# A fixed matmul order for the linear-recurrence stage of a hybrid diffusion layer

## The chip, the cores and the metric

The kernel runs on one core of a Trainium2 chip. The metric is the device time of one execution in microseconds (us); the time before is the median of three runs. Engines are named as the profile does: PE (TensorE matmul), PEld (TensorE weight load), DVE (VectorE), ACT (ScalarE), POOL (GpSimd), SP (the queue that issues DMAs).

## The reference

One transformer-like layer (DEPTH 1, model width 1024) is applied to 128 context tokens and 512 latent tokens that share all weights, so T = 640 tokens. A combined input projection feeds four mixers; the first, an HGRN2 gated linear recurrence in both directions with 4 heads of 128 x 128, is the one that this change is about:

```
q = silu(u['hgrn_q']); v = u['hgrn_i']; f = lb + (1 - lb) * sigmoid(f_pre); k = (1 - lb) * sigmoid(-f_pre)
# per chunk, b = cumsum(log f):
A = einsum('bthk,bshk,btshk->bhts', q, k, exp(b_t - b_s))       # s <= t
o = A @ v + (q * exp(b)) @ S
S = exp(b_last) * S + (k * exp(b_last - b))^T @ v
o = rmsnorm(o_fwd + o_bwd) * silu(u['hgrn_g'])
```

The other mixers are windowed attention, latent attention and grouped-query attention; each is projected to the model width, weighted by sigmoid gates of its own (a projection of 1024 columns per branch), and a squared-ReLU MLP follows. The final context states of the recurrence are outputs too.

## The kernel before, in words

All weights are split into a high part (fp32r) and a remainder, and so are the activations: a dense product is three matmuls. `t_block` (L322) makes a transposed block, 128 output channels by 640 tokens in two halves of 320, 8 x 3 matmuls per half (L330 to L332), in one of two `mm` PSUM buffers; `tok_block` (L335) makes a block of 128 tokens by 256 or 512 channels (L341 to L343). `wtile` (L289) loads a weight tile of 128 x 1024, copies its high part on POOL (`copy_r`, L124, tile wh) and subtracts on DVE (`rest`, L127, tile wl); raw, high and low parts have three buffers each.

The linear-recurrence stage works on two pairs of heads (hp = 0, 1), and all 640 tokens at once:

- `hgrn_project(hp)` (L406): the query projection (evacuated by L412 on ACT and L413 on DVE) and the forget gates of both directions (L423 and L424 on ACT, L426 and L430 on DVE, L428 on POOL). Six blocks of 48 matmuls.
- `hgrn_levels` (L437): the matrix A by recursion. It begins with QP = q * f (L441, DVE) and KS (L446, POOL) and a group of 32-wide blocks on PE (L459). Then for h = 1, 2, 4, 8, 16: a copy into KS on ACT (L468), a group of blocks (L459), and the update of the running products: QP on DVE (L485), the keys hk on POOL (L488, one per direction), the gates hf on DVE (L489); the blocks are merged under a mask (L491). For h = 32 and 64 the blocks are L478 and their results are copied to A (L495).
- `hgrn_out(hp, ...)` (L503): transposes of the keys (L515), copied by ACT (L517); the state updates u in groups of eight matmuls into two PSUM buffers (L522), chained on DVE (L527), with the final context state copied out by ACT (L530); the outputs po from A and the states (L543, L546, L547); squares (L551), the mean and its power -1/2 (L189, L190), the gated result (L559), its transposes (L561) and the split result (L566, L567).
- `hgrn_gate(hp)` (L583): the output gate, five `tok_block`s of 24 matmuls of 256 columns (L588, L589).
- `gates(n)` (L569): the branch gate, eight `t_block`s.

Blocks, key transposes and outputs share two `sc` PSUM buffers; the state updates and the result's transposes share two `tp` buffers. Behind the stage comes the windowed attention, whose key and value projections are `tok_block`s into `sc` buffers.

The order of instructions on each engine is chosen by a planner that simulates the program with a table of costs: at each moment it takes, among the instructions that are ready, the one of the highest priority, which is the order in which the program states them unless `high_priority` raises it. Tiles get a buffer when one is free. The stage is stated so:

```
qfk = hgrn_project(0)
lev = hgrn_levels(*qfk, hx)
qfk = hgrn_project(1)
hgrn_gate(0)
with tc.high_priority():
    hgrn_out(0, *lev, hV, hG, hx)
hgrn_gate(1)
sig0 = gates(0)
with tc.high_priority():
    lev = hgrn_levels(*qfk, hx)
    hgrn_out(1, *lev, hV, hG, hx)
```

Of the kernel before, what the change touches and what calls it, by code (L numbers as in the profile page):

```python
# [64 lines left out]
def trunk(ctx, tc, I, O):  # L65
    nc = tc.nc
    V, S, G, PE = nc.vector, nc.scalar, nc.gpsimd, nc.tensor
    dma = nc.sync.dma_start

# [219 lines left out]
    def wtile(rows, k0, c0, n, nk):  # L289
# [12 lines left out]
        copy_r(hi[:, 0:m], raw[:, 0:m])  # L302
# [3 lines left out]
    wtile.side = 0  # L306

# [98 lines left out]
    def hgrn_project(hp):  # L406
        qa = big(F32, 4, T, name="qA")
# [7 lines left out]
        fg = big(F32, 2, 2, T, name="hf")  # L415
        kk = big(F32, 2, 2, T, name="hk")
        for d, nm in enumerate(('hff', 'hfb')):
# [12 lines left out]
            V.tensor_scalar(out=fg[:, 1 - d], in0=fg[:, 1 - d], scalar1=LOG_FLOOR, scalar2=None, op0=ALU.max)  # L430
        return qa, fg, kk
# [5 lines left out]
    def hgrn_levels(qa, fg, kk, hx):  # L437
# [25 lines left out]
        flat = lambda x: lambda t: x.rearrange("p m t -> p (m t)")[:, t:t + 32]  # L463
        L = blocks(flat(KS), flat(q))
        V.tensor_tensor(out=AD, in0=L, in1=eye32.unsqueeze(1).to_broadcast([128, 10, 32]), op=ALU.mult)
        for li, h in enumerate(LEVELS):
            if h < 32:
                S.activation(out=skip(KS, 0, (2 * h, n2 // (2 * h)), (h, 2), (1, h)), in_=cross(kk, 0, n2 // (2 * h), h),  # L468
                             func=AF.Copy)
                L = blocks(flat(KS), lambda t: cross(QP, t, 16 // h, h))  # L470
            else:

                L = sc_tile()[:, :, 0:5 * h].rearrange("p m (c t) -> p m c t", t=h)
# [22 lines left out]
            if h == 16:  # L496
# [3 lines left out]
        return (qa, A, [QP[:, 1 - d] for d in range(2)], [kk[:, d] for d in range(2)],  # L500
                [[fg[:, 1 - d, m] for m in range(2)] for d in range(2)])

    def hgrn_out(hp, qa, A, QP, KR, P, hV, hG, hx):  # L503
        need = {0: [0, 1, 2, 4], 1: [3, 2, 1, 4]}
        st = hx.tile([128, 4, 4, 128], F32, tag="St", name="St")
        for d in range(2):
            for m in range(2):
                hd = 2 * hp + m
                dma(out=st[:, 2 * d + m, 0], in_=I['state_hgrn'][0, 0, d, hd])
        for d in range(2):  # L510
            kt_ps = sc_tile().rearrange("p m (j s) -> p m j s", j=4)
            kts = []
            for m in range(2):
                for j, c in enumerate(need[d]):
                    PE.transpose(out=kt_ps[:, m, j], in_=KR[d][:, m, 128 * c:128 * c + 128], identity=ident)  # L515
                kts.append(small(name="kt").rearrange("p (j s) -> p j s", j=4))
                S.activation(out=kts[m], in_=kt_ps[:, m], func=AF.Copy)  # L517
            for m in range(2):
                hd, kt = 2 * hp + m, kts[m]
# [5 lines left out]
                for j in range(3):  # L525
                    c = need[d][j]
                    V.scalar_tensor_tensor(out=s0[:, j + 1], in0=s0[:, j], scalar=P[d][m][:, 128 * c + 127 * d:128 * c + 127 * d + 1],  # L527
                                           in1=u[:, 128 * j:128 * j + 128], op0=ALU.mult, op1=ALU.add)
# [6 lines left out]
        on = qa[:, 0:2].rearrange("p m t -> p (m t)").rearrange("p (i v) -> p i v", v=128)  # L535
        for cs in ((4,), (0, 1, 2, 3)):
# [18 lines left out]
            for m in range(2):  # L555
                hd = 2 * hp + m
                tp = tp_tile()
                for i, c in enumerate(cs):
                    V.scalar_tensor_tensor(out=on[:, 2 * c + m], in0=po[:, 2 * i + m], scalar=r[:, 2 * i + m:2 * i + m + 1],  # L559
                                           in1=hG[:, c, 128 * hd:128 * hd + 128], op0=ALU.mult, op1=ALU.mult)  # L560
                    PE.transpose(out=tp[:, i], in_=on[:, 2 * c + m], identity=ident)  # L561
                gain = vcol[:, 40 + hd:41 + hd]
                t = slice(128 * cs[0], 128 * cs[-1] + 128)
                src = tp[:, 0:len(cs)].rearrange("p i t -> p (i t)")
                hi, lo = (x[:, t] for x in OT[0][hd])
                S.activation(out=hi, in_=src, func=AF.Copy, scale=gain)  # L566
                V.scalar_tensor_tensor(out=lo, in0=src, scalar=gain, in1=f(hi), op0=ALU.mult, op1=ALU.subtract)  # L567

    def gates(n):  # L569

# [11 lines left out]
    with tc.tile_pool(name="hx", bufs=1) as hx:  # L582
# [14 lines left out]
        with tc.high_priority():  # L597
            hgrn_out(0, *lev, hV, hG, hx)
# [590 lines left out]
```

## Time and profile before

| | |
|---|---|
| median of 3 runs | 1521.66 us (1520.61 to 1524.54) |
| the profiled execution | 1524.19 us, span 1522.4 us, mean granted clock 0.987 |
| PE busy | 1443.2 us, 95% of the span |
| PEld busy | 1309.7 us, 86% |
| DVE busy | 801.6 us, 53% |
| ACT busy | 459.8 us, 30% |
| POOL busy | 478.8 us, 31% |
| chain that ended last | PE 69%, issue 14%, DVE 7%, POOL 6%, DMA 2%, ACT 2% |

Busy is the time in which an engine has an instruction under way; a wait is the idle time just ahead of an instruction, put down to what released it. Matmuls overlap, so the start of one to the start of the next is the pace, and its own duration is longer. The granted clock is TensorE's, as a share of full speed.

### The profile page before, as it was taken

How to read it: one execution, taken by the hardware profiler on the slowest of the kernel's cores; microseconds unless marked ns; L12 is line 12 of the kernel's file. 1: busy time of each engine (PE TensorE's matmuls, PEld its weight loads, DVE VectorE, ACT ScalarE, POOL GpSimd, SP SyncE). 2: the span in 40 equal slices, each digit the busy share in tenths (PEclk: the TensorE clock that was granted, in tenths of full speed). 3: DMA queues.
4: the chain of work that ended last, by engine and by line, in shares of the span. 5: the costliest groups of instructions: out<-in, count | busy, mean ns of one | idle time of the engine just before them, and what ended most of it. 6: DMA issues, size and time to landing. Idle time of an engine off the chain costs nothing.

```text
span 1522.4 us, 26814 instructions
## 1 busy us (share of the span) xinstructions
PE 1443.2 (95%) x10970; PEld 1309.7 (86%) x10970; DVE 801.6 (53%) x1459; ACT 459.8 (30%) x1158; POOL 478.8 (31%) x506
## 2 busy tenths in 40 slices
PE   5998898999999899999998988998999999999996
PEld 3798898999899898899997677887897998998995
DVE  3337767347753497542734467756333444444446
ACT  3322232333434234442123565315220110110112
POOL 2226738232322344321323344124211112112114
PEclk9999999999999999999999999999999999999998
DMA  9422212223112230112323701231334132212221
GB/s 296 139 70 57 52 48 64 64 60 70 44 43 46 58 70 15 50 39 54 93 66 115 257 31 43 74 107 56 92 116 125 58 95 84 80 63 80 70 70 70
DMA packets 140410, 121.18 MB, mean 80 GB/s; under 512 B 22432, under 2 KB 121596, under 8 KB 140288
## 3 DMA queue, kind: packets, MB, share of 16 engines
q1 hardware_dynamic: 140288, 119.47, 27.0%
q8 instruction: 86, 1.41, 0.4%
q14 instruction: 36, 0.29, 0.1%
HBM read 115.96 MB, written 3.49 MB: 78 GB/s over the span
## 4 chain that ended last, share of the span: by engine, by line
PE 69%; issue 14%; DVE 7%; POOL 6%; DMA 2%; ACT 2%; SPq 0%; POOLq 0%; DVEq 0%; ACTq 0%
PE mm L330 11%; PE mm L331 11%; PE mm L332 11%; POOL wh L124 4%; PE mm L341 4%; PE mm L342 4%; PE mm L343 4%; PE tp L706 3%; PE sc L341 3%; PE pv L859 3%; PE sc L343 3%; PE sc L342 2%; PE sc L799 2%; PE sc L800 2%; DMA wada<-in_w_ada 1%
## 5 line engine op out<-in xcount | busy, mean ns | idle before, releaser
L124 POOL TENSOR_SCALAR wh<-wr 128x1024 fp32r<-128x1024 f32 (+3 forms) x161 | 193.4, 1203 | 583.1 <-PE mm L331 325.1
L127 DVE TENSOR_TENSOR wl<-wr,wh 128x1024 fp32r<-128x1024 f32 (+3 forms) x161 | 199.7, 1242 | 180.3 <-POOL wh L124 179.8
L330 PE MATMUL mm<-hTh,wh 128*128 128x320 f32 x704 | 221.9, 315 | 3.6 <-DVE qA L413 2.2
L332 PE MATMUL mm<-hTh,wl 128*128 128x320 f32 x704 | 221.9, 315 | 1.3 <-DVE wl L127 1.2
L331 PE MATMUL mm<-hTl,wh 128*128 128x320 f32 x704 | 220.6, 313 | 0.0
L331 PE MATMUL mm<-h2Tl,wh 128*128 128x320 f32 x512 | 159.3, 311 | 0.9 <-DVE h2Tl L127 0.9
L330 PE MATMUL mm<-h2Th,wh 128*128 128x320 f32 x512 | 159.2, 312 | 0.0
L332 PE MATMUL mm<-h2Th,wl 128*128 128x320 f32 x512 | 159.1, 311 | 0.0
L659 POOL TENSOR_SCALAR P<-P,rden 128x640 f32<-128x640 f32 (+3 forms) x120 | 83.2, 703 | 177.6 <-DVE rden L671 75.7
L330 PEld LDWEIGHTS mm<-hTh,wh 128*128 128x128 f32 x704 | 133.8, 190 | 5.8 <-DVE qA L413 2.3
L332 PEld LDWEIGHTS mm<-hTh,wl 128*128 128x128 f32 x704 | 133.8, 190 | 2.9 <-DVE wl L127 1.8
L331 PEld LDWEIGHTS mm<-hTl,wh 128*128 128x128 f32 x704 | 133.7, 190 | 0.7 <-issue 0.3
L342 PE MATMUL mm<-wl,hidh 128*128 128x512 f32 x320 | 124.7, 390 | 0.6 <-DVE wl L127 0.6
L341 PE MATMUL mm<-wh,hidh 128*128 128x512 f32 x320 | 125.3, 392 | 0.0
L343 PE MATMUL mm<-wh,hidl 128*128 128x512 f32 x320 | 124.5, 389 | 0.0
L1142 ACT ACTIVATE relu<-mm 128x320 f32<-128x320 f32 x64 | 28.0, 437 | 281.1 <-PE mm L332 281.0
L331 PEld LDWEIGHTS mm<-h2Tl,wh 128*128 128x128 f32 x512 | 97.0, 189 | 1.6 <-DVE h2Tl L127 1.3
L330 PEld LDWEIGHTS mm<-h2Th,wh 128*128 128x128 f32 x512 | 96.8, 189 | 0.7 <-issue 0.4
L332 PEld LDWEIGHTS mm<-h2Th,wl 128*128 128x128 f32 x512 | 97.0, 189 | 0.0
L1143 DVE TENSOR_TENSOR relu<-relu 128x320 f32<-128x320 f32 x64 | 40.3, 629 | 100.4 <-ACT relu L1142 100.4
L1155 DVE TENSOR_TENSOR y<-mm,y 128x512 f32<-128x512 f32 x70 | 48.2, 688 | 82.0 <-PE mm L343 82.0
L706 PE MATMUL tp<-ident,P 128*128 128x128 f32 x456 | 72.2, 280 | 3.2 <-DVE modcol L228 1.1
(350 smaller groups left out, 3251.8 us busy)
## 6 DMA issues: line engine op xcount, KB each, us to landing
wr<-in_w_in SPq DMA_DIRECT2D x55, 512.0 KB, 3.8
wada<-in_w_ada SPq DMA_DIRECT2D x44, 512.0 KB, 4.4
wr<-in_w_mlp_in SPq DMA_DIRECT2D x32, 512.0 KB, 4.0
wr<-in_w_mlp_out SPq DMA_DIRECT2D x32, 512.0 KB, 3.5
wr<-in_w_in SPq DMA_DIRECT2D x64, 64.0 KB, 2.1
wr<-in_w_branch SPq DMA_DIRECT2D x8, 512.0 KB, 3.5
wr<-in_w_branch SPq DMA_DIRECT2D x16, 256.0 KB, 4.0
wr<-in_w_out SPq DMA_DIRECT2D x8, 512.0 KB, 3.5
```

The source lines that it names most:

```text
L124: G.tensor_scalar(out=out, in0=src, scalar1=1.0, scalar2=1.0, op0=ALU.mult, op1=ALU.mult)
L127: V.tensor_tensor(out=out, in0=src, in1=f(hi), op=ALU.subtract)
L330: PE.matmul(out=ps[:, 0:tn], lhsT=wh, rhs=a, start=(k == 0), stop=False)
L331: PE.matmul(out=ps[:, 0:tn], lhsT=wh, rhs=b, start=False, stop=False)
L332: PE.matmul(out=ps[:, 0:tn], lhsT=wl, rhs=a, start=False, stop=(k == nk - 1))
L341: PE.matmul(out=ps[:, 0:n], lhsT=a, rhs=w[k][0], start=(start and k == 0), stop=False)
L342: PE.matmul(out=ps[:, 0:n], lhsT=a, rhs=w[k][1], start=False, stop=False)
L343: PE.matmul(out=ps[:, 0:n], lhsT=b, rhs=w[k][0], start=False, stop=(stop and k == nk - 1))
L659: G.tensor_scalar(out=Pt[:, i, 0:W], in0=Pt[:, i, 0:W], scalar1=rden[:, i:i + 1], scalar2=1.0, op0=ALU.mult, op1=ALU.mult)
L706: PE.transpose(out=tp[:, kk, i], in_=Pt[:, i, 128 * (kt + kk):128 * (kt + kk) + 128], identity=ident)
L859: PE.matmul(out=out, lhsT=Vt[:, ks[kt], 64 * a:64 * a + 64], rhs=PTa, start=start, stop=stop)
L1155: V.tensor_tensor(out=ys, in0=ps, in1=ys, op=ALU.add)
```

## The change

A wrapper around the matmul engine ties each matmul and transpose to the one stated before it while it is switched on, so that PE executes them in the order of the program. `hgrn_project`, `hgrn_levels`, `hgrn_out`, `hgrn_gate` and the branch gate (`gate_steps`) become generators: each `yield` is a place between two parts. One loop walks through the levels and the output of each pair of heads and, at each of their places, takes one step of a single stream of dense work: the projection of the second pair, both output gates, the branch gate. Matmuls that are stated behind the stage are not tied. Within the stage and in the first projection the high part of a weight is copied by ACT in place of POOL. The raised priorities are gone, and the tiles of the second projection are allocated ahead. In `hgrn_out` all key transposes come first (with the state's DMAs between them), and the result's transposes come after all products; L430 is done per direction as before, inside the second block's step.

```
+    class Ordered:
+        on = False
+        last = None
+        def tie(self, i):
+            if self.on and self.last is not None:
+                tc.add_manual_dep(i.ins, self.last.name, mybir.DependencyInfo(
+                    mybir.DependencyClass.NoSync, mybir.DependencyReason.DATA), reason="order")
+            self.last = i.ins
+            return i
+        def matmul(self, **kw):
+            return self.tie(nc.tensor.matmul(**kw))
...
-        copy_r(hi[:, 0:m], raw[:, 0:m])
+        if wtile.act:
+            S.activation(out=hi[:, 0:m], in_=raw[:, 0:m], func=AF.Copy)
+        else:
+            copy_r(hi[:, 0:m], raw[:, 0:m])
...
     # hgrn_project: a yield behind each of its six blocks
     # hgrn_levels:
+        yield
         L = blocks(flat(KS), flat(q))
...
             if h < 32:
                 S.activation(out=skip(KS, ...), in_=cross(kk, ...), func=AF.Copy)
+                yield
                 L = blocks(flat(KS), lambda t: cross(QP, t, 16 // h, h))
             else:
+                yield
                 L = sc_tile()[:, :, 0:5 * h].rearrange("p m (c t) -> p m c t", t=h)
...
     # hgrn_out: key transposes of both directions; yield; state updates; yield; outputs, squares,
     # products; yield; transposes of the results
...
     # hgrn_gate: a yield behind the second and the fifth tok_block
     # gate_steps: a yield behind each of its eight t_blocks
...
+        def dense():
+            yield from hgrn_project(1, *qfk[1])
+            for hp in range(2):
+                yield from hgrn_gate(hp)
+            sig0.extend(big(F32, 4, T, name="sig") for _ in range(2))
+            yield from gate_steps(0, sig0)
...
+        wtile.act = True
+        qfk, sig0 = [hgrn_tiles()], []
+        for _ in hgrn_project(0, *qfk[0]):
+            pass
+        OT[0] = []
+        qfk.append(hgrn_tiles())
+        PE.on = True
+        fill = dense()
+        for hp in range(2):
+            lev = hgrn_levels(*qfk[hp], hx)
+            while True:
+                try:
+                    next(lev)
+                except StopIteration as e:
+                    A, QP = e.value
+                    break
+                next(fill, None)
+            for _ in hgrn_out(hp, *qfk[hp], A, QP, hx):
+                next(fill, None)
+        for _ in fill:
+            pass
+        PE.on = False
+        wtile.act = False
```

## Rows read from the trace of the kernel before

**Rows 1.** Busy time by windows: the window (from, to and length in us), then busy us and instructions of PE, PEld, DVE, ACT and POOL, the granted clock, the DMA share and GB/s.
```profile
80.00:121.00 41.00, 41.00 (x281) 41.00 (x281) 15.11 (x16) 7.45 (x19) 13.39 (x11) 1.00 0.27 74
121.00:312.00 191.00, 174.82 (x2314) 168.80 (x2312) 124.48 (x148) 53.36 (x128) 103.43 (x58) 0.96 0.22 58
312.00:345.00 33.00, 33.00 (x275) 33.00 (x274) 17.60 (x38) 11.16 (x29) 12.87 (x18) 1.00 0.18 53
```

**Rows 2.** The waits of PE from 121 to 312 us: who waited for whom, us in total, times, longest us.
```profile
PE sc L459 <- DVE QP L485: 4.5, 2, 2.3
PE sc L459 <- ACT KS L468: 2.4, 2, 1.5
PE mm L330 <- DVE qA L413: 2.2, 1, 2.2
PE mm L341 <- DVE hG L589: 1.9, 1, 1.9
PE tp L561 <- DVE qA L559: 1.3, 1, 1.3
PE mm L332 <- DVE wl L127: 1.2, 1, 1.2
PE sc L478 <- DVE QP L485: 1.1, 1, 1.1
PE mm L330 <- DVE hG L589: 0.9, 1, 0.9
PE mm L330 <- ACT hk L424: 0.5, 1, 0.5
```

**Rows 3.** Busy time by windows (columns as in the first group) around four of these waits.
```profile
125.00:135.00 10.00, 7.82 (x190) 7.45 (x185) 4.17 (x5) 2.62 (x3) 3.62 (x2) 0.83 0.01 2
145.00:155.00 10.00, 7.71 (x119) 7.42 (x118) 7.69 (x6) 1.92 (x3) 6.83 (x3) 0.83 0.23 66
215.00:225.00 10.00, 8.74 (x139) 8.07 (x129) 5.97 (x14) 5.06 (x6) 4.58 (x3) 0.83 0.01 2
240.00:250.00 10.00, 7.75 (x118) 7.46 (x117) 6.78 (x6) 2.82 (x4) 7.39 (x4) 0.83 0.30 75
```

**Rows 4.** The timeline of PE, groups of blocks of the recursion: start and length in us, engine, line, operation, and in brackets the idle time before it and what ended it.
```profile
133.93 1.06 PE L459 MATMUL sc<-QP,KS 128*32 128x32 f32 x80
139.66 0.90 PE L459 MATMUL sc<-QP,KS 128*32 128x32 f32 x80
...
149.23 1.30 PE L459 MATMUL sc<-QP,KS 128*32 128x32 f32 x80 [2.29 <-DVE QP L485]
...
235.46 0.90 PE L459 MATMUL sc<-QP,KS 128*32 128x32 f32 x80
243.88 0.94 PE L459 MATMUL sc<-QP,KS 128*32 128x32 f32 x80 [2.25 <-DVE QP L485]
```

**Rows 5.** Groups of instructions from 121 to 170.5 us, the copies of weights on POOL: busy us and mean ns of one, then the idle time before them.
```profile
L124 POOL TENSOR_SCALAR wh<-wr 128x1024 fp32r<-128x1024 f32 x4 | 9.7, 2423 | 4.7 <-PE mm L331 4.7
```

**Rows 6.** Instructions by line over the whole span: durations in ns (shortest, median, longest), first and last start, shapes; the last row is one of the page's groups (busy us, mean ns of one).
```profile
L488 POOL TENSOR_TENSOR hk<-hk,hf x28: 1278/1860/3107, 127.8 to 266.4; 128x640 f32<-128x640 f32 x28
L485 DVE TENSOR_TENSOR QP<-QP,hf x14: 1492/2454/3109, 135.1 to 265.2; 128x1280 f32<-128x1280 f32 x14
L489 DVE TENSOR_TENSOR hf<-hf x14: 200/773/3147, 138.0 to 269.5; 128x1280 f32<-128x1280 f32 x2, 128x640 f32<-128x640 f32 x2, 128x320 f32<-128x320 f32 x2, 128x160 f32<-128x160 f32 x2
L468 ACT ACTIVATE KS<-hk x10: 1269/1274/1843, 125.9 to 249.1; 128x1280 f32<-128x1280 f32 x10
L127 DVE TENSOR_TENSOR wl<-wr,wh 128x1024 fp32r<-128x1024 f32 (+3 forms) x161 | 199.7, 1242 | 180.3 <-POOL wh L124 179.8
```

**Rows 7.** The timeline around the last two levels of the second pair of heads (columns as in the fourth group).
```profile
256.50 0.90 PE L478 MATMUL sc<-QP,hk 128*32 128x32 f32 x80
...
262.07 0.33 PE L478 MATMUL sc<-QP,hk 128*64 128x64 f32 x2
...
263.11 1.38 PE L478 MATMUL sc<-QP,hk 128*64 128x64 f32 x38
...
264.53 4.39 POOL L488 TENSOR_TENSOR hk<-hk,hf 128x640 f32<-128x640 f32 x2 [0.50 <-PE sc L478]
```

**Rows 8.** The timeline of a state update of the first pair: the matmuls, the chain on DVE, the copy of the final state.
```profile
199.45 1.06 PE L522 MATMUL pv<-hV,kt 128*128 128x128 f32 x8
...
200.54 1.11 DVE L527 SCALAR_TENSOR_TENSOR St<-St,hf,pv 128x128 f32<-128x128 f32 x3 [0.42 <-PE pv L522]
...
201.82 0.28 ACT L530 ACTIVATE fin<-pv 128x128 f32<-128x128 f32 x1 [2.16 <-DVE St L527]
```

**Rows 9.** The timeline behind the outputs of the second pair: the last output matmuls, and the gated products.
```profile
297.77 0.39 PE L547 MATMUL sc<-St,QP 128*128 128x128 f32 x2
...
302.35 2.16 DVE L559 SCALAR_TENSOR_TENSOR qA<-sc,rs,hG 128x128 f32<-128x128 f32 x8 [1.77 <-POOL rs L190]
```

**Rows 10.** Groups of instructions of PE from 420 to 480 us, in the windowed attention (columns as in the fifth group): one of the three lines of the branch gate's matmuls, and the attention's transposes.
```profile
L331 PE MATMUL mm<-hTl,wh 128*128 128x320 f32 x89 | 27.6, 310 | 0.0
...
L706 PE MATMUL tp<-ident,P 128*128 128x128 f32 x48 | 8.0, 281 | 0.0
```

**Rows 11.** The timeline of PE in the key and value projections of the windowed attention: two matmuls of 256 columns, with five between them.
```profile
312.26 0.28 PE L343 MATMUL sc<-wh,hTl 128*128 128x256 f32 x1
...
312.97 0.28 PE L343 MATMUL sc<-wh,hTl 128*128 128x256 f32 x1
```

More of the change, by code (lines that the diff above doesn't have):

```diff
@@ L499, in hgrn_levels, with hgrn_out @@
                     S.activation(out=A[r, :, r], in_=AD[r], func=AF.Copy)
-        return (qa, A, [QP[:, 1 - d] for d in range(2)], [kk[:, d] for d in range(2)],
-                [[fg[:, 1 - d, m] for m in range(2)] for d in range(2)])
-    def hgrn_out(hp, qa, A, QP, KR, P, hV, hG, hx):
+        return A, [QP[:, 1 - d] for d in range(2)]
+    def hgrn_out(hp, qa, fg, KR, A, QP, hx):
         need = {0: [0, 1, 2, 4], 1: [3, 2, 1, 4]}
         st = hx.tile([128, 4, 4, 128], F32, tag="St", name="St")
+        kts = []
+        for d in range(2):
+            kt_ps = sc_tile().rearrange("p m (j s) -> p m j s", j=4)
+            for m in range(2):
+                dma(out=st[:, 2 * d + m, 0], in_=I['state_hgrn'][0, 0, d, 2 * hp + m])
+                for j, c in enumerate(need[d]):
+                    PE.transpose(out=kt_ps[:, m, j], in_=KR[:, d, m, 128 * c:128 * c + 128], identity=ident)
+                kts.append(small(name="kt").rearrange("p (j s) -> p j s", j=4))
+                S.activation(out=kts[-1], in_=kt_ps[:, m], func=AF.Copy)
+        yield
         for d in range(2):
             for m in range(2):
[L508 to L519, printed above, removed]
+                hd, kt = 2 * hp + m, kts[2 * d + m]
                 u = pv_tile()
@@ L525, in hgrn_out @@
                 for j in range(3):
[L526 to L527 removed]
+                    t = 128 * need[d][j] + 127 * d
+                    V.scalar_tensor_tensor(out=s0[:, j + 1], in0=s0[:, j], scalar=fg[:, 1 - d, m, t:t + 1],
                                            in1=u[:, 128 * j:128 * j + 128], op0=ALU.mult, op1=ALU.add)
@@ L535, in hgrn_out @@
         on = qa[:, 0:2].rearrange("p m t -> p (m t)").rearrange("p (i v) -> p i v", v=128)
+        yield
+        ready = []
         for cs in ((4,), (0, 1, 2, 3)):
@@ L560, in hgrn_out, with gate_steps @@
                                            in1=hG[:, c, 128 * hd:128 * hd + 128], op0=ALU.mult, op1=ALU.mult)
[L561 to L569, printed above, removed]
-        sig = [big(F32, 4, T, name="sig") for _ in range(2)]
+                ready.append((hd, m, cs))
+        yield
+        for hd, m, cs in ready:
+            tp = tp_tile()
+            for i, c in enumerate(cs):
+                PE.transpose(out=tp[:, i], in_=on[:, 2 * c + m], identity=ident)
+            gain = vcol[:, 40 + hd:41 + hd]
+            t = slice(128 * cs[0], 128 * cs[-1] + 128)
+            src = tp[:, 0:len(cs)].rearrange("p i t -> p (i t)")
+            hi, lo = (x[:, t] for x in OT[0][hd])
+            S.activation(out=hi, in_=src, func=AF.Copy, scale=gain)
+            V.scalar_tensor_tensor(out=lo, in0=src, scalar=gain, in1=f(hi), op0=ALU.mult, op1=ALU.subtract)
+    def gate_steps(n, sig):
         for kk in range(8):
@@ L579, in gates @@
                 S.activation(out=g, in_=g, func=AF.Sigmoid)
+            yield
+    def gates(n):
+        sig = [big(F32, 4, T, name="sig") for _ in range(2)]
+        for _ in gate_steps(n, sig):
+            pass
         return sig
```

34 lines of the change are left out of this document (15 added, 19 removed).

## The prediction

> **What bounds the kernel now.** I read the share of busy time by engine first, then the busy time by windows, then who waits for whom on TensorE, then the timeline around those waits. TensorE works almost without a break before and after the linear-recurrence stage; the stage itself, 121 to 312 us, is where it is not full: it is busy 174.8 of 191 us at a granted clock of 0.96, and 33.0 of 33 us right behind [rows 1]. So 16.2 us of idle time can be won there, and no more than that but for the clock. The list of TensorE's waits in that stretch has nine lines which sum to 16.0 us [rows 2]: 8.0 at the blocks of the recursion (4.5 and 1.1 for the product into QP, L485; 2.4 for the copy into KS, L468), 2.2 for the evacuation of a query block (L413), 2.8 for the evacuation of the output gate (L589), 1.3 for the normalised output (L559), 1.2 for a weight remainder (L127), 0.5 for L424. The clock costs something beside it: four stretches of 10 us, each around such a wait, ran at 0.83, which is a mix of the 1.2 and 2.4 GHz levels and costs up to 1.7 us each, 6.8 together [rows 3].
>
> Why the levels wait is seen in the timeline. From the start of one group of blocks to the next it takes 8.4 to 9.6 us where TensorE waited for L485 (139.66 to 149.23, 235.46 to 243.88) [rows 4]. The planner reckons with less: between 134.99, where one group ended, and 139.66 it had put 4.7 us of dense matmuls. POOL has a part in the long spans: four copies of weights took 2.42 us each in the first 50 us of the stage, 9.7 us in all [rows 5].
>
> **The change part by part.** All sums are made against the profiled execution, 1524.19 us (span 1522.4, 1.8 around it). It stands 2.5 us above the median of 1521.66, to which I carry the difference over.
>
> *The fixed order.* Each level is followed by one dense step: 48 matmuls of 320 columns, 7.0 us at 281 in 41.0 us [rows 1], or, for the output gate, 48 and 72 of 256 columns at 0.118 (six in 0.71) [rows 11], 5.7 and 8.5 us. With the blocks' own 0.9 us [rows 4] a level then recurs after about 8 us, and the dense part is 7.0 us instead of 4.7. That covers the spans above, so I take the level waits as gone (8.0), with them those for L589, L127 and L424 (2.8, 1.2, 0.5): 12.5 us. Two of the clock dips go with their waits (145 to 155 and 240 to 250): 3.4. Two waits stay, with their dips: the 2.2 us for L413, because the first level still queues the long product L441 on VectorE ahead of that evacuation, and the 1.3 us before L561, since one step of 7.0 us lies where the chain from the last output matmul takes about as long. **Removed: 15.9 us.** The number of matmuls stays.
>
> *What the new order exposes for the first pair of heads.* Between the blocks of level 64 and the transposes of the keys no step is put. The transposes need POOL's last pair of products, L488, which begins as the blocks end and takes 4.4 us [rows 7]; now dense matmuls lie there. The first eight transposes need one half of it only and fill 0.9 (eight matmuls of the state updates, 1.06 with the overlap of the last) [rows 8], so I charge 4.4 - 0.9 = 3.5. The state updates come in groups of eight matmuls into two buffers; one is free 1.6 us after its group's end (L527 1.11 us, then L530, done at 202.10 after a group that ended at 200.5), a group lasts 0.9, so the third and fourth group wait 0.7 and 0.3: 1.0. **Added: 4.5 us.** A bound below is 0 for the 1.0, if VectorE is ahead; above, the 4.4 in full.
>
> *What it exposes for the second pair.* There are 18 dense steps (6 projections, 4 half gates, 8 branch gates) and 22 places (11 per pair). The first pair takes 11, the second has 7: its places 8 to 11 are empty. Level 64 then follows level 32 directly: 257.40 to 262.07, 4.7 us [rows 7]; the transposes 3.5 and the state groups 1.0 as above; the last state update before the outputs 0.4; and behind the outputs the squares, the power on POOL and L559, from 298.16 to 302.35, 4.2, and some 1.2 more because L559 paces the transposes (2.16 us for eight) [rows 9]. That is 15.0 us of TensorE time, which gate matmuls cover now.
>
> *What can fill it.* The order binds only the stage's matmuls; those of the next branch are free, and the planner does draw later work forward: the gate matmuls at 420 to 480 us (89 on one of their three lines) stand in the program behind the attention whose transposes they lie between [rows 10]. Ready in time are the key and value projections, 24 matmuls or 2.8 us per token tile [rows 11]. Each needs one of the two sc buffers, which the blocks and outputs also use. I take one tile in the hole before level 64, one before the transposes, and 4.2 us behind the outputs: 2.9 + 2.9 + 4.2 = 10.0, and 5.0 stay open. **Added: 5.0 us**, between 0 (all filled) and 15.0 (none). I choose this value since the timeline shows such filling wherever the planner has ready work, but never with both sc buffers under dispute.
>
> *The clock* after the new holes: between none and two dips (3.4); I take half of one, 0.8, because the holes that stay are short beside those of [rows 3].
>
> *The weight copies* (1024 columns) go from POOL to ScalarE: 24 tiles. By ScalarE's copy of 1280 columns, 1.27 us, I estimate 1.0 us each [rows 6]. ScalarE is busy 53 of 191 us [rows 1], so it holds them; queued behind them are the evacuations, and a late one is covered by the second mm buffer, worth 3.5 us. If that cover fails the price is at most 1 us a time. POOL is rid of 9.7 us in the first half, which is why I do not charge the levels with lateness. The other edits I cost at nothing: the four state DMAs are the same, their buffer is free since level 16, and what stands behind them on SP's queue are weight tiles that are wanted a step or two later; tiles allocated earlier and the raised priorities taken out only order what the dense steps hide. Without that cover each shows as a wait like the 0.5 for L424 [rows 2]; planned anew, these may move the sum by 1 to 3 us either way.
>
> **Sum:** -15.9 + 4.5 + 5.0 + 0.8 = -5.6, so 1521.66 - 5.6 = 1516.1 us.
>
> **The rivals.** *The empty end (slower).* The planner fills nothing in places 8 to 11, because the outputs and blocks hold both sc buffers: -15.9 + 4.5 + 15.0 + 3.4 = +7.0, 1528.7 us. It decides when less than about 5 us is filled. For it: no row shows the projections drawn into this place, TensorE was full there. Against it: [rows 10]. Chance 0.19.
>
> *VectorE and POOL set the pace (no change).* A level's products are long when they meet: L485 takes 1.49 to 3.11 us, L488 1.28 to 3.11 [rows 6]. If they must take turns, a level costs at the shortest 1.49 + 0.77 (L489, median) + 2 x 1.28 + 1.24 (L127) = 6.1, and the first pair has the products L426, L428 and L430 beside it, so a step of 8 us has hardly a reserve. Half of the level waits (4.0) and one dip (1.7) would stay: -5.6 + 5.7 = +0.1, 1521.8 us. Chance 0.2. The Trainium skill (SBUF — State Buffer, section Who interferes with whom) says just this, that a VectorE instruction with two inputs in SBUF and a GpSimd one that reads SBUF exclude each other for a whole instruction; the stretched durations agree, but moving the weight copies off POOL then helps too, so the rule speaks on both sides.
>
> *Everything fits.* The holes fill whole and the first wait goes with its dip: -15.9 - 3.9 + 4.5 = -15.3, 1506.4 us. Chance 0.11. That the order is not kept is excluded: it is a dependency from each matmul to the one before.
>
> **How the numbers follow.** My forecast has 0.5. About 0.3% (4.6 us) is what a measurement of this kernel tells from no change; the forecast lies 1.0 us beyond it, with a spread of some 4 us from the planner, so I give 0.34 of its 0.5 to faster and 0.16 to the same. With the good case and a little of the others: faster 0.47, same 0.34, slower 0.19. The range runs from the good case to the empty end: 1506 to 1528.5; the forecast alone is 1512 to 1521.
>
> **What would show it.** Right: no TensorE wait for L485 or L468 between 130 and 250 us; a wait for L488 ahead of the transposes, 2 to 4 us, in both pairs; matmuls of the key projection (line L341's group into sc) between the last blocks and the last transposes of the second pair; ScalarE about 24 us busier, POOL as much less. Wrong: an unfilled stretch of over 10 us after level 32 of the second pair, or the level waits still there at the end of 7 us steps.

## The result, and the profile after

The changed kernel takes 1533.96 us (median of 4 runs, 1533.25 to 1535.55) against 1521.13 us of the kernel before in the same comparison (4 runs, 1519.91 to 1524.54): **ratio 1.0082, 95% interval 1.0064 to 1.0100: slower, by less than 1%.** The prediction was 1516.1 us, faster; the time lies above its range of 1506 to 1528.5. The profiled execution took 1534.07 us (span 1532.1), 9.9 more than the one before (1524.19).

Nearly all of it arises in the stage. A mark behind the stage and the first attention is the load of the second attention's cached keys; a mark further on is the store of the third one's latent keys. The timeline of SyncE's queue, the kernel before and then the changed one (start and length in us, queue, line, operation):

```profile
407.00 0.34 SPq L724 DMA_DIRECT2D ctxk<-in_cache_gqa_k  x1
...
773.92 0.36 SPq L930 DMA_DIRECT2D out_mla_ckv<-mtx  x1
```

```profile
416.27 0.34 SPq L785 DMA_DIRECT2D ctxk<-in_cache_gqa_k  x1
...
784.74 0.36 SPq L991 DMA_DIRECT2D out_mla_ckv<-mtx  x1
```

The first mark is 9.3 us later, the second 10.8. To see where in the stage, I cut it into four: the levels of the first pair of heads, its end (transposes of the keys, state updates, outputs, normalisation), the levels of the second pair, and its end. TensorE's windows, before and after (window, length, busy us and instructions, granted clock, DMA share, GB/s):

```profile
121.00:180.00 59.00, 49.20 (x849) 0.94 0.19 53
180.00:240.00 60.00, 55.87 (x728) 0.97 0.19 46
240.00:290.00 50.00, 47.76 (x577) 0.97 0.31 78
290.00:322.00 32.00, 32.00 (x249) 1.00 0.21 54
```

```profile
121.00:180.00 59.00, 56.81 (x903) 0.97 0.25 69
180.00:240.00 60.00, 50.81 (x391) 0.89 0.19 49
240.00:290.00 50.00, 50.00 (x780) 1.00 0.26 65
290.00:322.00 32.00, 22.58 (x249) 0.73 0.12 36
```

I call *lost* the length of a window less busy time times granted clock, that is, idle time and slow clock in one number (the clock's two digits make it good to some 0.3 us a window). Before: 12.8, 5.8, 3.7, 0.0; 22.2 in all. After: 3.9, 14.8, 0.0, 15.5; 34.2 in all. So **both sets of levels became as full as was forecast, which won 12.5 us, and both ends lost more than that: 9.0 in the first pair, 15.5 in the second.** In the whole stage, the answer to [rows 1] is:

```profile
121.00:312.00 191.00, 170.37 (x2233) 163.84 (x2232) 115.10 (x127) 66.01 (x118) 73.03 (x39) 0.91 0.22 58
```

ScalarE (66.01) is 12.7 us busier than before there and POOL 30.4 less. TensorE's waits from 100 to 345 us, the answer to [rows 2] (the first six lines; who waited for whom, us in total, times, longest):

```profile
PE sc L86 <- POOL hk L518: 5.2, 2, 2.7
PE sc L83 <- DVE QP L515: 5.2, 1, 5.2
PE tp L86 <- DVE o L601: 3.8, 1, 3.8
PE sc L86 <- ACT kt L543: 3.5, 5, 0.8
PE mm L83 <- DVE qA L440: 2.2, 1, 2.2
PE pv L83 <- ACT fin L558: 0.9, 2, 0.7
```

In the new program all matmuls have the line L83 and all transposes L86; QP is L515 (L485 before), hk L518 (L488), the copy of the transposed keys L543 (L517), the remainder of the split result L601 (L567), which frees the tp buffer that the next transposes write. The copies into KS have gone from the list, and of the five waits for QP and KS one is left, in a place without a dense step. The other lines, but for L440, are the ends of the two pairs. The timeline there, the first pair's transposes and then the second pair's last two levels and transposes, with VectorE and POOL beside them (in brackets the idle time before a row and what ended it):

```profile
188.66 0.89 PE L86 MATMUL sc<-ident,hk 128*128 128x128 f32 x4 [2.50 <-POOL hk L518]
190.24 1.12 PE L86 MATMUL sc<-ident,hk 128*128 128x128 f32 x4 [0.69 <-ACT kt L543]
192.13 1.08 PE L86 MATMUL sc<-ident,hk 128*128 128x128 f32 x4 [0.78 <-ACT kt L543]
193.91 1.12 PE L86 MATMUL sc<-ident,hk 128*128 128x128 f32 x4 [0.69 <-ACT kt L543]
...
291.01 0.90 PE L83 MATMUL sc<-QP,hk 128*32 128x32 f32 x80
291.02 1.05 POOL L144 TENSOR_SCALAR wh<-wr 128x1024 fp32r<-128x1024 f32 x1 [6.85 <-PE mm L83]
292.10 2.31 DVE L147 TENSOR_TENSOR wl<-wr,wh 128x1024 fp32r<-128x1024 f32 x1 [4.65 <-POOL wh L144]
294.33 2.58 DVE L515 TENSOR_TENSOR QP<-QP,hf 128x1280 f32<-128x1280 f32 x1
297.06 2.40 PE L83 MATMUL sc<-QP,hk 128*64 128x64 f32 x40 [5.15 <-DVE QP L515]
302.19 1.11 PE L86 MATMUL sc<-ident,hk 128*128 128x128 f32 x4 [2.73 <-POOL hk L518]
...
319.71 0.36 PE L83 MATMUL sc<-wh,hTh 128*128 128x256 f32 x1
```

Three things are to be seen. The transposes of the first pair come in fours, and each four waits for the copy of the four ahead of it. Between 291.91 and 319.71 TensorE has only the recursion itself: the first matmul of the next branch's key projection (the last row, into an sc tile) stands behind the outputs. And the same 40 blocks of level 64 that take 1.39 us at full clock (run e8 below) take 2.40 here.

### The profile page after: what moved, and what is told of

It is laid out like the page before. It is cut to its first block, busy times and chain, and to the rows that moved or that the text cites. A ratio compares the mean times of both kernels' runs of the same rounds, so it can differ in the third digit from the quotient of the medians.

```text
span 1532.1 us, 26813 instructions
## 1 busy us (share of the span) xinstructions
PE 1450.2 (95%) x10970; PEld 1316.0 (86%) x10970; DVE 798.6 (52%) x1459; ACT 486.4 (32%) x1182; POOL 437.2 (29%) x482
## 4 chain that ended last, share of the span: by engine, by line
PE 73%; issue 12%; DVE 6%; POOL 4%; ACT 2%; DMA 2%; SPq 0%; POOLq 0%; DVEq 0%; ACTq 0%
PE mm L83 48%; PE sc L83 14%; PE pv L83 4%; PE tp L86 4%; POOL wh L144 3%; DVE wl L147 1%; DMA wada<-in_w_ada 1%; PE ada_ps L83 1%; PE sc L86 1%; PE tp L83 0%; DMA wr<-in_w_in 0%; ACT P L730 0%; PE pj L83 0%; DVE y L1153 0%; POOL hk L518 0%
## 5 line engine op out<-in xcount | busy, mean ns | idle before, releaser
L144 POOL TENSOR_SCALAR wh<-wr 128x1024 fp32r<-128x1024 f32 (+3 forms) x137 | 158.0, 1155 | 525.7 <-PE mm L83 481.9
L147 DVE TENSOR_TENSOR wl<-wr,wh 128x1024 fp32r<-128x1024 f32 (+3 forms) x161 | 200.6, 1248 | 194.8 <-POOL wh L144 141.1
L83 PE MATMUL mm<-hTh,wh 128*128 128x320 f32 x704 | 221.3, 314 | 2.2 <-DVE qA L440 2.2
L83 PE MATMUL mm<-hTh,wl 128*128 128x320 f32 x704 | 220.5, 313 | 0.0
L83 PE MATMUL mm<-hTl,wh 128*128 128x320 f32 x704 | 219.3, 312 | 0.0
L83 PE MATMUL mm<-h2Tl,wh 128*128 128x320 f32 x512 | 159.1, 311 | 0.3 <-DVE h2Tl L147 0.3
L83 PE MATMUL mm<-h2Th,wh 128*128 128x320 f32 x512 | 159.3, 312 | 0.0
L83 PE MATMUL mm<-h2Th,wl 128*128 128x320 f32 x512 | 158.9, 310 | 0.0
L83 PEld LDWEIGHTS mm<-hTh,wh 128*128 128x128 f32 x704 | 133.4, 189 | 3.9 <-DVE qA L440 2.3
L83 PEld LDWEIGHTS mm<-hTh,wl 128*128 128x128 f32 x704 | 133.3, 189 | 1.1 <-issue 0.7
L83 PEld LDWEIGHTS mm<-hTl,wh 128*128 128x128 f32 x704 | 133.3, 189 | 0.5 <-issue 0.3
L83 PE MATMUL mm<-wl,hidh 128*128 128x512 f32 x320 | 124.7, 390 | 0.6 <-DVE wl L147 0.6
L83 PE MATMUL mm<-wh,hidh 128*128 128x512 f32 x320 | 125.2, 392 | 0.0
L83 PE MATMUL mm<-wh,hidl 128*128 128x512 f32 x320 | 124.6, 389 | 0.0
L83 PEld LDWEIGHTS mm<-h2Tl,wh 128*128 128x128 f32 x512 | 96.8, 189 | 1.0 <-DVE h2Tl L147 0.7
L83 PEld LDWEIGHTS mm<-h2Th,wh 128*128 128x128 f32 x512 | 96.9, 190 | 0.7 <-issue 0.4
L83 PEld LDWEIGHTS mm<-h2Th,wl 128*128 128x128 f32 x512 | 96.8, 189 | 0.0
L83 PE MATMUL sc<-wh,hTh 128*128 128x256 f32 (+2 forms) x224 | 72.9, 326 | 3.2 <-DVE tx L846 2.4
```

Of the source, the lines that this page charges most:

```text
L83: return self.tie(nc.tensor.matmul(**kw))
L144: G.tensor_scalar(out=out, in0=src, scalar1=1.0, scalar2=1.0, op0=ALU.mult, op1=ALU.mult)
L147: V.tensor_tensor(out=out, in0=src, in1=f(hi), op=ALU.subtract)
```

## The experiments

One line a run, each against the kernel before in the same comparison, whose median lay between 1521.1 and 1523.3 us; so runs of different comparisons are set side by side by their ratios, and *us* is the ratio less 1, times 1522. *Lost* is the sum over the four windows above, spare work counted as busy (an estimated 7.3 us in e8 and 2.6 in e13, whose *lost* is that much too good).

| run | edit | median us | ratio (95% interval) | us | lost us | first mark us |
|---|---|---|---|---|---|---|
| before | | 1521.1 to 1523.3 | 1 | 0 | 22.2 | 407.0 |
| after | the change | 1533.96 | 1.0082 (1.0064 to 1.0100) | +12.5 | 34.2 | 416.3 |
| e1 | keys into mm | 1526.82 | 1.0026 (1.0015 to 1.0036) | +4.0 | 27.1 | 410.2 |
| e2 | order free | 1518.85 | 0.9971 (0.9958 to 0.9984) | -4.4 | 18.4 | 396.4 |
| e3 | copies on POOL | 1541.47 | 1.0117 (1.0101 to 1.0132) | +17.8 | 40.4 | 422.3 |
| e4 | first pair fixed | 1520.92 | 0.9988 (0.9978 to 0.9999) | -1.8 | 21.0 | 400.8 |
| e5 | e2 + e1 | 1511.11 | 0.9924 (0.9909 to 0.9939) | -11.6 | 10.8 | 394.1 |
| e6 | e4 + e1 | 1521.17 | 0.9990 (0.9979 to 1.0001) | -1.5 | 21.0 | 402.3 |
| e7 | before, copies on ACT | 1519.47 | 0.9977 (0.9965 to 0.9989) | -3.5 | 17.3 | 401.4 |
| e8 | after, spare work | 1533.22 | 1.0071 (1.0056 to 1.0086) | +10.8 | 22.3 | 412.7 |
| e9 | more dense steps | 1536.95 | 1.0096 (1.0079 to 1.0113) | +14.6 | 27.9 | moved |
| e10 | e1 + batched transposes | 1525.26 | 1.0018 (1.0009 to 1.0028) | +2.7 | 20.2 | 404.1 |
| e11 | e9, all covered | 1521.82 | 0.9991 (0.9978 to 1.0003) | -1.4 | 13.5 | moved |
| e12 | e5 + batched transposes | 1509.30 | 0.9911 (0.9896 to 0.9925) | -13.5 | 9.5 | 393.2 |
| e13 | after, spare work in first pair | 1534.62 | 1.0078 (1.0063 to 1.0094) | +11.9 | 29.6 | 415.6 |
| e14 | e10, first pair covered | 1523.37 | 1.0001 (0.9991 to 1.0011) | +0.2 | 21.2 | 403.4 |

**Why nothing was drawn into the empty places (e1).**

```
-            ps = tok_block(wk, 256, hT, tt, sc_bank())
+            ps = tok_block(wk, 256, hT, tt, mm_tile() if n == 1 else sc_bank())
```

> One edit to the changed kernel: the key and value projection of the next branch (first such branch only) writes its sums into the ring of the mm tiles, which the dense steps leave free at 291 us, and no longer into the ring of the two sc tiles, which the last blocks, key transposes and outputs hold in turn. Theory A (the empty places stayed empty because the next branch's first matmuls stood in line for an sc tile): two token tiles (5.6 us of matmuls) go in between the last blocks and the key transposes of the second pair, the wait for QP (5.2) goes, the clock dip of 290 to 300 shrinks by 2 to 3; 1525 to 1528 us against 1534. Theory B (the tail is not what costs, the first pair and the copies on ScalarE are): 1531 or more.

Measured: 1526.82 us, the time that theory A named, and by the ratios 8.5 less than the changed kernel. Two of its waits from 240 to 330 us (same columns):

```profile
PE sc L86 <- POOL hk L518: 2.3, 1, 2.3
...
PE sc L83 <- DVE QP L515: 0.2, 1, 0.2
```

The wait for QP fell from 5.2 to 0.2: 40 matmuls of the key projection now lie between level 32 and level 64 and 8 behind level 64. So work and weights were there. What was missing was the buffer: the two sc tiles are handed out in the order of the program, and the blocks, key transposes and outputs of the second pair stand ahead of the next branch in it.

**The order itself (e2, e4).** e2 leaves out the line `PE.on = True`. e4 ends the fixed order behind the first pair, lets the remaining gate steps stand free and raises the priority of the second pair:

```
+        pair(0, lambda: next(fill, None))
+        PE.on = False
+        for _ in fill:
+            pass
+        with tc.high_priority():
+            pair(1, lambda: None)
```

> The changed kernel without the dependency between successive matmuls: the same program text, tiles, weight copies on ScalarE and priorities, but the planner orders TensorE. Theory A (the fixed order with its four empty places is what costs): the holes of the second pair fill with dense steps, the level waits come back; 1518 to 1525 us. Theory B (something else in the rewrite costs: the copies on ScalarE, the raised priorities taken out, the tiles taken early): 1530 or more with the order free too.

> The changed kernel with the order fixed for the first pair of heads alone; for the second pair the seven branch-gate steps that are left stand free and the recursion has the raised priority, as in the kernel before. Theory A (the loss lies in the second pair's empty places and the half clock behind them): most of the 9.4 us comes back, 1521 to 1526 us, with no TensorE hole above 3 us between 290 and 320. Theory C (the first pair's transposes, their serial copies and the half clock cost as much): 1528 to 1532.

By time both went as theory A has it: 1518.85 us, and 1520.92, just below its range. e2's program differs from the changed one in the dependency alone, so **the fixed order costs 16.9 us by the ratios, and without it the rest of the change is faster than the kernel before.** The windows of e2 and, without the first, of e4:

```profile
121.00:180.00 59.00, 56.82 (x904) 0.97 0.25 68
180.00:240.00 60.00, 60.00 (x636) 1.00 0.25 62
240.00:290.00 50.00, 42.00 (x670) 0.90 0.24 65
290.00:322.00 32.00, 30.00 (x251) 0.99 0.07 18
```

```profile
180.00:240.00 60.00, 54.65 (x646) 0.91 0.20 50
240.00:290.00 50.00, 46.40 (x628) 0.93 0.26 62
290.00:322.00 32.00, 32.00 (x264) 1.00 0.13 40
```

e2 shows two things I had not expected. With the order free the levels of the first pair are as full as with the order fixed (56.82 and 56.81 of 59), and its end is full as well; the level waits that I expected back did not come. And the second pair has the same hole with the order free (its wait for QP is 5.2 us too): the planner had used up the dense steps, and the next branch stood in line for an sc tile here as well. So theory A's mechanism, steps that fill the second pair's holes, is not what happened in e2. By the windows its gain lies in the first pair's end, which loses nothing (14.8 us with the order fixed), while its second pair (240 to 322 us) loses 14.5 instead of 15.5. In e4, whose second pair is free and has priority, that pair loses 6.8 and the first pair's end 10.3. Which place a hole falls to is the plan's choice; that the fixed order costs, both runs show. The hole that e2 leaves is what e1's edit should mend.

**The weight copies (e3, e7).** e3 leaves out `wtile.act = True`; e7 is the kernel before with that one switch.

> The changed kernel with the weight copies back on POOL, the fixed order kept. Theory A (order and empty places cost, not the copies): the holes stay and POOL, 24 x 2.4 us busier, is late with its halves of the key products; 1534 to 1540 us. Theory B (the copies on ScalarE delay the evacuations of transposes and outputs): the waits for the key transposes' copies on ScalarE (3.5 us) shrink, 1527 to 1531.

> The kernel before with one part of the change alone: the weight copies of the stage on ScalarE. Theory A (POOL's copies are part of the long level spans; the copies off POOL are what the free order of e2 gains): 1517 to 1520 us. Theory B (the copies matter only where the order is fixed and a late weight cannot be passed by; e2's gain comes from the steps and the priorities): 1521 to 1524.

e7 went as theory A has it. e3 lies 1.5 us above theory A's range, and for another reason than the one named: TensorE's wait for POOL's keys did not grow (4.6 us, 5.2 in the changed kernel), but it waits 2.7 us for weights (L144, L147) and 3.2 for a copy of blocks on VectorE (L525). The copies on ScalarE are a gain by themselves: 3.5 us in the kernel before, and 5.3 by the ratios with the order fixed (1.0117 to 1.0082). ScalarE's copy takes 1.06 us; POOL's had taken 2.42 in the first 50 us of the stage [rows 5], but 1.05 from 249 us to its end. From 121 to 312 us of the changed kernel (busy us, mean ns, then idle time before):

```profile
L323 ACT ACTIVATE wh<-wr 128x1024 fp32r<-128x1024 f32 x15 | 15.9, 1059 | 20.1 <-PE mm L83 20.1
```

e2 and e7 have intervals that overlap, so by time the rest of the rewrite (steps, no raised priority) cannot be told from nothing; by the first mark it is worth 5.0 us (401.4 to 396.4), which e2 loses again later: between the two marks it takes 372.7 us, the kernel before 366.9.

**Both together, and the best (e5, e6, e12).**

> The order left free, and the next branch's key projection in the ring of the mm tiles: the edits of the runs e2 and e1 together. Theory A (matmuls of the next branch stand in line for an sc tile, with or without the fixed order): the hole that the free order left in the second pair at 275 to 290 us (8 of 20 us idle, granted clock 0.52 behind it) takes two or three token tiles; 1512 to 1515 us. Theory B (the planner would not draw them in here): 1518 us or more, as with the free order alone.

> The order fixed for the first pair alone, as in the run e4, and the key projection in the mm ring. Theory A (with free branch gates and the raised priority the second pair has no hole, so there is nothing for the key projection to fill): 1519 to 1522 us, the same as e4. Theory B (the key projection is worth 7 us wherever it stands, as in the fixed order): 1514 to 1516.

e5 took 1511.11 us, a little better than theory A named, and e6 the same as e4, as expected. The reason given does not quite hold: in both the second pair waits 3.6 us for the copy into KS, and the key projection is not drawn in there; no run shows why. e12 adds to e5 the transposes of a direction issued as eight, with the two copies behind them (the edit of e10):

```
             for m in range(2):
                 dma(...)
                 for j, c in enumerate(need[d]):
                     PE.transpose(out=kt_ps[:, m, j], ...)
+            for m in range(2):
                 kts.append(...)
                 S.activation(out=kts[-1], in_=kt_ps[:, m], func=AF.Copy)
```

> The fastest so far (order free, key projection in the mm ring, e5) with the batched transposes: its waits for the transposes' copies are 1.5 us. 1508 to 1511 us; or 1511 to 1512 if the wait only moves to the state updates.

1509.30 us: faster than both kernels, by 0.9% and 1.7%; from e5 its ratio's interval is not apart. The lost time of the stage is 9.5 us instead of 22.2 and 34.2.

**Half clock or idle time (e8, e13).** Spare matmuls into an mm tile, in the fixed order (e8: 32 ahead of the second pair's level 64 and 18 ahead of its transposes; e13: 18 ahead of the first pair's transposes):

```
+            ps = mm_tile()
+            for k in range(n):
+                PE.matmul(out=ps[:, 0:320], lhsT=hT[0][0][:, 0:128], rhs=hT[k % 8][0][:, 0:320], ...)
```

> The changed kernel with spare work in two of its holes, in the fixed order: 32 matmuls of 320 columns (4.7 us at full clock) between level 32 and level 64 of the second pair, and 18 (2.6 us) between level 64 and the key transposes; their sums are read by nothing. Theory A (behind the holes TensorE runs at the lower of its two clock levels and that costs as much again): 7.3 us more of work and a shorter time, 1527 to 1530 us, with a granted clock near 1.00 at 300 to 310 instead of 0.50. Theory B (the time is set by the chain over VectorE, POOL and ScalarE, and the clock is only a sign of the idle time): 1533 to 1536.

> The changed kernel with spare work in the first pair's one place without a step: 18 matmuls of 320 columns (2.6 us) between level 64 and the key transposes; their sums are read by nothing. Theory A (the hole of 2.5 us is charged twice, once as idle time and once as half clock on the 10 us of dense work behind it, granted clock 0.54): the granted clock of 190 to 200 us is over 0.9, the second pair begins 3 to 4 us earlier, 1530 to 1532 us. Theory B (the chain over POOL and ScalarE sets the time, the clock costs nothing): the second pair begins at the same time or later, 1534 to 1536.

In the stage e8 went as theory A has it, in the time as theory B. TensorE's windows, the changed kernel and then e8:

```profile
295.00:300.00 5.00, 2.40 (x40) 0.50 0.35 108
300.00:305.00 5.00, 2.13 (x9) 0.50 0.00 0
```

```profile
295.00:300.00 5.00, 4.71 (x64) 1.00 0.32 105
300.00:305.00 5.00, 2.99 (x22) 1.00 0.00 0
```

With the holes full of work that nobody needs, the same blocks and transposes ran at 2.4 GHz (granted clock 1.00) and not at 1.2 (0.50), and the first mark came 3.6 us earlier (416.3 to 412.7). So some 3.6 us of the second pair's end are the clock's own, as far as this run separates it from the idle time. The whole time is only 1.7 us lower by the ratios, and their intervals overlap: between the marks e8 takes 370.8 us and the changed kernel 368.5, and behind the second mark the profiled execution is no shorter. In the attention between them a matmul waits 3.4 us for VectorE's product with a branch gate, where the changed kernel waits 2.0. With every edit the planner orders the later branches anew; over all runs, the stretch between the marks took from 366.8 to 372.7 us in the kernels that leave the gates in their place. That sets how finely a median speaks of the stage.

e13's theory A failed: its first mark is 0.7 us earlier, not 3 to 4, and the clock of 190 to 200 us rose to 0.83, not above 0.9. The wait for POOL went, but the fours of transposes with 0.7 to 0.9 us between them stayed, and the clock fell behind them.

**What the transposes in fours cost (e10).**

> The run e1 (key projection in the mm ring, fixed order) with the key transposes of a direction issued as eight and the two copies to SBUF behind them, in place of four, copy, four, copy. Theory A (each group of four waits for the copy of the group ahead of it, which I had left out): the waits for the copies, 3.5 us in both pairs, fall to 1.5 or less, and the half clock behind them is shorter; 1523 to 1526 us against 1526.8. Theory B (the copies are waited for in any case, by the state updates): 1526 to 1528.

The waits for their copies fell from 3.5 to 1.2 us in both pairs together, and the second pair's end, 290 to 322 us, lost 3.4 us where e1 lost 8.4. That is more than the waits: e1's granted clock there is 0.84, e10's 1.00, though both wait 2.3 us for POOL just before. The first mark is 6.1 us earlier; 1525.26 us lies at theory A's upper end and only 1.2 below e1 by the ratios, which their intervals do not tell apart; this plan takes 3.9 us more between the marks.

**Can the fixed order be mended (e9, e14, e11)?** e9 puts the second branch's gates into the list of steps; e14 (on e10, in the first pair alone) and e11 (on e9, in both pairs, with the transposes batched) add a place ahead of the key transposes:

```
             yield from gate_steps(0, sig0)
+            sig1.extend(big(F32, 4, T, name="sig") for _ in range(2))
+            yield from gate_steps(1, sig1)
...
         need = {0: [0, 1, 2, 4], 1: [3, 2, 1, 4]}
+        yield
```

> The changed kernel, fixed order, with eight more dense steps: the gates of the second branch (56 us of matmuls that stood behind its attention) are put at the end of the list of steps, so that the places 8 to 11 of the second pair have work; the four steps that are left follow the stage. Theory A (the loss of the fixed order is its empty places): the waits of the second pair for QP (5.2 us) and its dips at 290 to 310 go, but for the transposes' wait for POOL (2.7); TensorE is busy 178 to 182 us of 121 to 312 instead of 170; 1522 to 1527 us, if the attention keeps its pace without those gates. Theory E (the gates are missed in the attention as much as they help here): busy as above in the stage, but 1531 or more in all. Theory B (the tail is slow for another reason): busy 172 or less.

> The run e10 (fixed order, key projection in the mm ring, batched transposes) with a place for a dense step between level 64 and the key transposes of the first pair; the second pair has one step less then. Theory A (a step at that place saves 2.5 us of waiting and 3 of half clock, and the second pair's level 32 now lacks a step, which the key projection fills in part): 1520 to 1524 us against 1525.3. Theory F (18 steps do not go round: the hole only moves to the second pair, whose levels wait some 5 us each without a step): 1525 to 1530.

> The fixed order with every hole found so far covered: the eight more steps of the run e9, a place with a step of its own between level 64 and the key transposes of both pairs, and the transposes batched as in e10. Theory A: no TensorE wait for POOL's products hk and none for QP between 121 and 312 us, a granted clock of 0.97 or more, busy 183 us or more; 1512 to 1519 us, if the attention keeps its pace. Theory E (the gates are missed in the attention): the stage as full as that, 1521 or more in all.

e9 is no gain: 1536.95 us. Its wait for QP is gone, TensorE is busy 175.1 us of 121 to 312 (between what A and B named), and the second pair's end still lost 9.2; the gates, which had lain between the attention's transposes [rows 10], are missing there: from 345 to 785 us TensorE waits 17.3 us, leaving out what still belongs to the stage (L601), where the changed kernel waits 10.5. Theory E holds for the time. e14's first pair lost 7.6 us at its end instead of e10's 12.9, and its second pair 9.8 instead of 3.4; 1523.37 us lies in theory A's range, 2.6 below e10 by the ratios (the ends of their intervals overlap), but in the stage theory F holds: the hole moved (20.2 and 21.2 us lost in all). In e11 the waits from 121 to 330 us are down to

```profile
PE pv L83 <- ACT fin L560: 4.2, 2, 2.1
PE tp L86 <- DVE o L603: 3.8, 1, 3.8
PE mm L83 <- DVE qA L440: 2.2, 1, 2.2
```

and the time is 1521.82 us, 16.0 below e9 by the ratios and no different from the kernel before: theory E again. So this fixed order with work in every place of the stage, taken from the second branch, reaches what the kernel before had, but 12.2 us more than what the free order reaches (e12) by giving the next branch a buffer. A fixed order filled with other work was not run.

## Why the prediction was wrong

I set the forecast out as lost time by window: what a window lost before, less the waits and dips taken off there, and what was added. That leaves 3.4 us in the levels, 7.5 in the first pair's end and 5.8 in the second's; measured are 3.9, 14.8 and 15.5. So both ends were priced too low, not the second alone.

*What bounds the kernel* and **the levels**: right. The levels' lost time went from 12.8 and 3.7 to 3.9 and 0.0 us, and what stays in the first pair is the wait of 2.2 us that I said would stay (L413 then, L440 now) with its dip. The waits for L589, L127 and L424 went too. But the fixed order was not needed for this: e2 has the first levels just as full (e7, with the copies alone, loses 11.1 us there).

**What can fill it: the step that failed.** Of 15.0 us of exposed time in the second pair I took 10.0 as filled by the next branch's key projection, reasoning from [rows 10]. The 4.2 behind the outputs came true: the projection runs from 319.71 us, right behind them. The two token tiles ahead of the transposes, 5.8 us, did not: nothing was filled there, and where the sum has 5.0 us open TensorE idled 9.4 (290 to 322 us). I had named both sc buffers as "under dispute" and still counted on them. The gates of [rows 10] go into mm tiles and were no evidence for a matmul into an sc tile. e1, which changes only that buffer, shows the cause: two token tiles went in at once, for 8.5 us less by the ratios.

**The clock: mis-sized, and in the windows the largest miss.** I took 0.8 us beside the two dips that stay. In the windows, busy time at less than full clock costs 5.6 us in the first pair's end (50.81 x 0.11) and 6.1 in the second's (22.58 x 0.27); the kernel before had 1.7 and none there. Over the whole stage it is 13.4 us, where my terms leave some 4 (6.8 - 3.4 + 0.8). Of the second pair's 6.1, e8 shows 3.6 us in the first mark; e13 did not separate the first pair's. I had charged dips only to holes, and not to the short waits behind them.

**The first pair: mis-sized.** I added 4.5 us, left the wait ahead of the output's transposes at 1.3, and so had 5.8 idle. Idle time at its end is 9.2 us against 4.1 before. Of my terms, 3.5 for POOL's hk measured 2.5, and 1.0 for the state updates measured 0.7 here (0.2 in the second pair). What I missed are the serial copies of the transposes (2.2 us here, 1.4 in the second pair; e10) and the wait for L601, 3.8 us. The second is an order on VectorE:

```profile
221.81 2.82 DVE L468 TENSOR_TENSOR QP<-qA,hf 128x2560 f32<-128x2560 f32 x1 [1.70 <-PE sc L83]
221.91 5.55 POOL L473 TENSOR_TENSOR KS<-hk 128x1280 f32<-128x1280 f32 x1 [2.45 <-PE sc L83]
224.55 2.93 DVE L209 TENSOR_SCALAR ms<-ssq 128x8 f32<-128x8 f32 x1
229.25 2.16 DVE L588 SCALAR_TENSOR_TENSOR qA<-sc,rs,hG 128x128 f32<-128x128 f32 x8 [1.77 <-POOL rs L210]
231.33 1.22 DVE L147 TENSOR_TENSOR wl<-wr,wh 128x1024 fp32r<-128x1024 f32 x1
232.46 0.60 DVE L601 SCALAR_TENSOR_TENSOR o<-tp,vcol,o 128x128 fp32r<-128x128 f32 x2
232.86 1.56 PE L86 MATMUL tp<-ident,qA 128*128 128x128 f32 x8 [3.83 <-DVE o L601]
```

The next pair's first products, QP (L468) and KS (L473), stand between the squares and the normalisation (L588), and a weight remainder (L147) ahead of L601. From the last output matmul (221.77) to the transposes (232.86) the chain takes 11 us where one dense step covers 7. The kernel before had the same collision (its L189 took 2.93 us too) and hid all but 1.3 us of it behind gate matmuls; a fixed order with one step at that place did not.

**The weight copies**: each costs ScalarE 1.06 us (1.0 estimated), with no evacuation late; 15 of the 24 lie between 121 and 312 us, so ScalarE is 12.7 us busier there and not the 24 that I named. I took them as no gain of their own; e3 and e7 show 5.3 and 3.5 us.

**The rivals.** *The empty end* happened in three of its four places (the one behind the outputs was filled), for the reason that I had named, and I gave it 0.19. Its 1528.7 us were still 5 too low: it charges 15.0 us for the second pair's idle time, which was 9.4, and too little for the clock and the first pair. *VectorE and POOL set the pace* did not decide the levels: with a dense step behind each, TensorE waits for none of their products there. The products remained as slow as in [rows 6] (QP 2.57 us in the median, hk 1.85), so a dense step of 7 us covers them even so. *Everything fits* did not happen.

What stays open: how the 14.8 us of the first pair's end divide into clock and idle time in the whole program's time; the 3 us by which the medians differ more (12.8) than the two profiled executions (9.9), which the interval of the ratio spans; and what of the medians of single edits is the stage and what a new plan behind it.

## What to carry to other kernels

Before counting on a planner to draw later work into a hole, look which buffer that work writes and who holds it in program order: one ring of PSUM tiles shared by two stages cost 8.5 us here (e1). An order written by hand must have work for every place, the short serial chain at the end above all; count steps against places first, and price an empty place at its idle time plus the slow clock behind it. A change of several parts can hide a gain: here the copies on ScalarE were faster than before (e7), the whole rewrite without the dependency too (e2), and the dependency was slower.

## What the runs showed of the hardware

A VectorE operation on 128x8 numbers (L209) took 2.93 us; the same one in the second pair took 0.17 (at 321.98). In the rows of the first pair above, VectorE's QP runs from 221.81 to 224.63 us, POOL's KS from 221.91 to 227.46, and L209 from 224.55 to 227.48. QP took 2.82 us also at 123.92, where POOL had nothing to do; KS took 3.09 at 120.11. So these times fit engines that took turns for whole instructions, KS behind QP and then the tiny L209 behind KS. The Trainium skill (SBUF — State Buffer, section Who interferes with whom) says that a VectorE instruction with two SBUF inputs, or one in a two-port mode, and a GpSimd instruction that reads SBUF exclude each other, and that whichever is issued first holds the ports to its end. The rows of QP and KS agree; L209 has one input, and no row shows in which mode it ran.

TensorE's clock fell to its lower level (1.2 GHz) also where no wait just before was longer than 0.9 us. In e13 TensorE has no wait from 180 us up to the transposes at 189.93, and the clock of 180 to 190 us is 1.00; then come transposes with waits of 0.69, 0.91 and 0.69 us, of which the rows of the first two follow, and TensorE's windows there:

```profile
191.22 0.65 PE L86 MATMUL sc<-ident,hk 128*128 128x128 f32 x4 [0.69 <-ACT kt L543]
192.78 0.63 PE L86 MATMUL sc<-ident,hk 128*128 128x128 f32 x4 [0.91 <-DVE qA L525]
```

```profile
192.00:194.00 2.00, 0.63 (x4) 1.00 0.13 37
194.00:196.00 2.00, 1.90 (x11) 0.65 0.00 0
196.00:198.00 2.00, 2.00 (x11) 0.50 0.00 0
```

The slow stretch, from 194 us on, lies behind the waits, mostly on dense matmuls; at 198 to 200 us the clock is 1.00 again. In e14 the same 16 transposes ran as one group of 1.91 us between two dense steps, and the granted clock stayed 1.00.
